# Scores in an attention block: the keys' low parts as one zero-padded matmul, or as two of 64 rows with a PSUM bank per pair of heads

## The chip, the cores and the metric

The kernel runs on one core of a Trainium2 chip. The metric is the device time of one execution in microseconds, the median of several runs. The core has TensorE (matmuls; its weight loads are shown as an engine of their own, PEld, beside PE), VectorE (DVE), ScalarE (ACT), GpSimd (POOL) and SyncE (SP), which here only issues DMAs.

## What is computed

One decoder layer for 512 tokens of width 4096: an RMS norm, one projection to queries (64 heads of 64), keys and values (8 heads of 64) and a gate (4096 wide), attention in a window of 128 tokens with a sink per head, the gate, an output projection, a residual and a final norm.

```python
h = rms_norm(x, norm_g)
q, k, v, z = split(h @ w_in + b_in)              # 4096, 512, 512, 4096 columns
s = einsum(q, k) * 64 ** -0.5                    # each query block of 128 against its own and the block before
s = where(0 <= i_q - i_k < 128, s, -inf)
m = max(max(s), sink)
p = exp(s - m) / (sum(exp(s - m)) + exp(sink - m))
x = x + ((p @ v) * silu(z)) @ w_out + b_out
out = rms_norm(x, final_g)
```

All of it is float32. The kernel's matmuls take operands in the format `fp32r`; it splits each operand into a high part (rounded to `fp32r`) and a low part (the rest), and sums three products: high x high, high x low, low x high.

## The kernel before

**Stages.** The input projection runs over 72 tiles of 128 output columns: for each of the 8 groups one tile with a key and a value head (`kv`), four with queries (`q0` to `q3`, two heads each) and four with the gate (`z0` to `z3`). A tile `acc` is 128 columns x 512 tokens in one PSUM bank and takes 32 steps over the 4096 inputs with three matmuls of 512 columns each (`mm_tile`, all through the helper `mm` at line 97). Weights come by DMA from SyncE's queue and are split on ScalarE and VectorE (`split`, lines 128 and 129). Then the output projection runs over 8 blocks of 512 columns, with the final norm behind it.

**Attention between the projection's matmuls.** The attention of a group is worked off while the projection of the following tiles runs. `tick()` is called after every chunk of 12 projection matmuls, and work that `at()` put down for that tick is issued there. All matmuls are kept in the order in which the program issues them (`tc.keep_in_program_order`), so TensorE's order is written out by hand. `quad` handles two query tiles, that is four heads in two pairs, and puts down for each of the four blocks of 128 tokens (n = 0 to 3): `scores` (three ticks apart), three ticks later `turn` (transposes of the probabilities), and two ticks after that `attend` (the product with the values). So `turn` of a block stands directly ahead of `scores` of the next block in one tick. There are 8 groups x 2 quads x 4 blocks = 64 calls of `scores`.

**The operands of the scores.** `q_tile` makes, from two heads in 128 rows, the tile `q2`: for head h one half of the rows holds the high part and the other half the low part (128 rows, per 64 tokens and head). `qq` collects high parts alone: rows 0 to 63 those of the first query tile of the quad (pair a = 0), rows 64 to 127 those of the second (a = 1). `kv_tile` makes `kh`, the keys' high part, in both halves of the rows, and `kl`, their low part: `kl[0:64, 0]` and the same values in `kl[64:128, 1]`, while the other two quarters hold zeros, written once by two memsets at the start (lines 272 and 273). `kl` is one tile for the whole kernel.

**A call of `scores`.** For each half-block u of 64 queries, the weights are `q2[a]` of 128 rows x 128 columns (two heads x 64 queries), for a = 0 and 1, with `kh` moving: that gives q_high x k_high and q_low x k_high in one matmul. Then one matmul with `qq` as weights and `kl` moving, over both its planes, adds q_high x k_low for both pairs: plane a meets zeros in the rows of the other pair. The result `ps` is 128 x 2 x 2 x 256, two PSUM banks, one per half-block u, both pairs in it. The window of keys has 192 columns, and 64 and 128 in the first block. After it VectorE brings the window into place (`copy_predicated`), takes the maximum, and ScalarE forms the exponentials. `ps` has one buffer.

Of each matmul the chip shows a weight load (LDWEIGHTS, on PEld) and the matmul itself.

Of the kernel before, what the change touches and what calls it, by code (L numbers as in the profile page):

```python
# [8 lines left out]
F32 = mybir.dt.float32  # L9
F32R = mybir.dt.float32r  # L10
I32 = mybir.dt.int32
AF = mybir.ActivationFunctionType
ALU = mybir.AluOpType
AX = mybir.AxisListType

P = 128
D = 4096
S = 512
HD = 64
# [8 lines left out]
QH = P // 2  # L28
# [14 lines left out]
def hybrid_block_kernel(  # L43
# [13 lines left out]
    nc = tc.nc  # L57
# [14 lines left out]
    for h in range(2):  # L72
        rows = mask[h * QH:(h + 1) * QH, 0]
# [22 lines left out]
    def mm(*a, **k):  # L96
        tc.keep_in_program_order(nc.tensor.matmul(*a, **k))  # L97

    def tr(*a, **k):
        tc.keep_in_program_order(nc.tensor.transpose(*a, **k))  # L100
# [5 lines left out]
    def at(slot, fn):  # L106
        clock[1] += 1
        due.append((slot, clock[1], fn))
# [51 lines left out]
    def split_w(raw, j):  # L160
        hi = wpool.tile([P, CW], F32R, name="whi", tag="whi", bufs=WB)
        lo = wpool.tile([P, CW], F32R, name="wlo", tag="wlo", bufs=WB)
        latest[1:] = split(raw[:, j], hi, lo)
        return hi, lo


    with ExitStack() as ph:
        att = ph.enter_context(tc.tile_pool(name="att", bufs=1))
        ps_s = ph.enter_context(tc.tile_pool(name="ps_s", bufs=1, space=PS))
# [76 lines left out]
        def scaled(acc, tag="tmp"):  # L246
            t = att.tile([P, S], F32, name=tag, tag=tag, bufs=1 if tag == "z" else 2)
            nc.vector.tensor_tensor(t, acc, rbc, op=ALU.mult)  # L248
            return t
# [18 lines left out]

        NW = S // QH + 1

        kl = att.tile([P, 2, S], F32R, name="kl")
        nc.vector.memset(kl[0:HD, 1].bitcast(F32), 0.0)
        nc.vector.memset(kl[HD:P, 0].bitcast(F32), 0.0)

        def kv_tile(g, acc):
            t = g * TPG
            b = bcol[:, t:t + 1]
            tmp = scaled(acc)
            kh = att.tile([P, S], F32R, name="kh", tag="kh", bufs=1)
            nc.scalar.activation(kh[0:HD], tmp[0:HD], AF.Identity, bias=b[0:HD])  # L280
            nc.vector.scalar_tensor_tensor(
                kl[0:HD, 0], tmp[0:HD], b[0:HD], kh[0:HD].bitcast(F32), op0=ALU.add, op1=ALU.subtract
            )
            nc.scalar.copy(kh[HD:P], kh[0:HD].bitcast(F32))
            nc.vector.tensor_copy(kl[HD:P, 1], kl[0:HD, 0].bitcast(F32))
            vT = att.tile([P, S], F32, name="vT", tag="tmp", bufs=2)
            nc.scalar.activation(vT, tmp, AF.Identity, bias=b)


            vv = att.tile([P, NW, 2, HD], F32R, name="vv", tag="vv", bufs=1)  # L290
            vw = att.tile([P, NW - 1, 2, HD], F32R, name="vw", tag="vw", bufs=1)
            lo, hi = slice(0, QH), slice(QH, P)

            def values():
                kv = ps_t.tile([P, NB, P], F32, name="pv", tag="pt")
                for n in range(NB):
                    tr(kv[:, n, :], vT[:, n * P:(n + 1) * P], ident)
                pv = kv[:, :, HD:]
                nc.gpsimd.memset(vv[lo, 0].bitcast(F32), 0.0)
                vh, vl = (vv[:, 1::2, i, :] for i in range(2))  # L300
                nc.scalar.copy(vh, pv)
                nc.vector.tensor_tensor(vl, pv, vh.bitcast(F32), op=ALU.subtract)
                nc.gpsimd.tensor_copy(vv[lo, 2::2], vv[hi, 1::2].bitcast(F32))
                nc.gpsimd.tensor_copy(vv[hi, 0:NW - 1:2], vv[lo, 1::2].bitcast(F32))
                nc.gpsimd.tensor_copy(vw[lo], vv[lo, 1:].bitcast(F32))
                nc.gpsimd.tensor_copy(vw[hi], vv[hi, :NW - 1].bitcast(F32))

            at(clock[0] + 1, values)
            return kh, vv, vw
# [28 lines left out]
        def scores(pair, n, q2, qh, kh):  # L338

            ps = ps_s.tile([P, 2, 2, 2 * P], F32, name="ps")
            for u in range(2):
                t0 = n * P + u * QH
                k0 = max(t0 - P, 0)
                o = ps[:, u, :, k0 - (t0 - P):QH + P]
                ks = slice(k0, t0 + QH)  # L350
                for a in range(2):
                    mm(o[:, a], q2[a][:, 2 * n + u], kh[:, ks], start=(a == 0), stop=False)
                mm(o, qh[:, 2 * n + u], kl[:, :, ks], start=False, stop=True)
            if n == 0:
                for u in range(2):
                    nc.vector.memset(ps[:, u, :, 0:P - u * QH], BIG)
            nc.vector.copy_predicated(
                ps[:, :, :, 0:QH], mask.bitcast(I32).unsqueeze(1).to_broadcast([P, 2, 2, QH]),
                ps[:, :, :, P:QH + P],
            )  # L360
            hs = slice(pair, pair + 2)
            nm = small.tile([P, 2, 2], F32, name="nm", tag="nm", bufs=2)
            nc.vector.tensor_reduce(nm, ps[:, :, :, 0:P], axis=AX.X, op=ALU.max, negate=True)
            nc.vector.scalar_tensor_tensor(  # L364
                nm, nm, SCALE, nsink[:, :, hs], op0=ALU.mult, op1=ALU.min
            )
            es = small.tile([P, 2, 2], F32, name="es", tag="es", bufs=2)
            nc.vector.tensor_tensor(es, nm, sink[:, :, hs], op=ALU.add)
            pr = att.tile([P, 2, 2, P], F32, name="prob", tag="prob", bufs=1)
            den = small.tile([P, 2, 2], F32, name="den", tag="den", bufs=2)  # L370
            for u in range(2):
                for a in range(2):
                    nc.scalar.activation(  # L373
                        pr[:, u, a, :], ps[:, u, a, 0:P], AF.Exp, bias=nm[:, u, a:a + 1],
                        scale=SCALE, accum_out=den[:, u, a:a + 1],
                    )
            nc.scalar.activation(es, es, AF.Exp)
            nc.vector.tensor_tensor(den, den, es, op=ALU.add)
            nc.vector.reciprocal(den, den)
            for u in range(2):  # L380
                for a in range(2):
                    nc.vector.tensor_scalar_mul(pr[:, u, a, :], pr[:, u, a, :], den[:, u, a:a + 1])
            return pr
# [43 lines left out]
        def quad(g, i, q2, qh, kh, vv, vw):  # L427
# [5 lines left out]
            def first(n):  # L433
                prs[n] = scores(g * 4 + 2 * i, n, q2, qh, kh)
# [62 lines left out]
        def evacuate(t, acc):  # L497
            g, i = divmod(t, TPG)
            if TILES[i] == "kv":
                kv[0] = kv_tile(g, acc)  # L500
                return
            p = int(TILES[i][1])
            if TILES[i][0] == "q":
                qs.append(q_tile(g, p, acc))
                if p % 2:
                    quad(g, p // 2, (qs.pop(0), qs.pop(0)), qq[0], *kv[0])
            else:
                gate(g, p, acc)
# [22 lines left out]
        for kc, t in ((kc, t) for kc in range(1, NC) for t in range(NPRE)):  # L531
            k2, i = divmod(kc, 2)
            raw = load_w(w_in[t, k2, :, i * CW:(i + 1) * CW], half=i)
            w = split_w(raw, i)
# [114 lines left out]
    for cc in range(NCC):  # L649
# [6 lines left out]
        for kt in range(HOLD, KT) if last else ():  # L656
# [6 lines left out]
            w = held[kt // 2][:, kt % 2]  # L663
            split(raw[:, kt % 2], w[:, 0], w[:, 1])
        for tb in range(NB):
            for kt in range(HOLD, KT) if last else ():
                w = held[kt // 2][:, kt % 2]
# [55 lines left out]
```

## Time and profile before

| | |
|---|---|
| runs | 2414.47, 2414.7, 2414.8 us; median 2414.7 |
| profiled execution | 2414.5 us, its span 2412.5 us, granted clock 0.998 |
| TensorE (PE) | busy 2396.6 us, 99%, 11025 matmuls |
| weight loads (PEld) | busy 1997.2 us, 83% |
| VectorE | busy 1404.3 us, 58% |
| ScalarE | busy 994.0 us, 41% |
| GpSimd | busy 326.1 us, 14% |
| DMA | 274.69 MB, mean 114 GB/s |

The span runs from the first instruction to the last of the profiled execution. Busy time of an engine is the time in which at least one of its instructions is under way; matmuls overlap in a pipeline and their ends are modelled, so starts say more than durations do. Times without a unit in the rows below are microseconds, those of single instructions in a group nanoseconds.

### The profile page before, as it was taken

Reading aid. Unit: us, or ns where it says so; the run is one execution under the profiler, and the core shown is the slowest. Engines: PE = TensorE matmul, PEld = TensorE weight load, DVE = VectorE, ACT = ScalarE, POOL = GpSimd, SP = SyncE. Lnnn points to the kernel's source line nnn. Section 1 sums busy time; section 2 is a strip of 40 time slices with the busy share of each in tenths; the row PEclk is TensorE's granted clock in tenths of the full one; section 3 lists DMA queues with packets and bytes.
Section 4 is the critical chain, followed back from the end, with each engine's and each line's share of the span. In section 5 each row is a group of like instructions: output and inputs, shape, how many; then the busy total and the mean of one; then the engine's idle time right before and its main releaser. Section 6 shows DMA issues by size and latency. Waiting matters only on the chain.

```text
span 2412.5 us, 30330 instructions
## 1 busy us (share of the span) xinstructions
PE 2396.6 (99%) x11025; PEld 1997.2 (83%) x11025; DVE 1404.3 (58%) x2514; ACT 994.0 (41%) x2146; POOL 326.1 (14%) x454
## 2 busy tenths in 40 slices
PE   9999999999999999999999999999999999999998
PEld 7888888888888888888888888888888888888886
DVE  5666465555646555564655556465764664665565
ACT  6643334343433434343343434334444444444444
POOL 2121011110101111010111101010210110110110
PEclk9999999999999999999999999999999999999999
DMA  9522222323232232333222233333632333333335
GB/s 310 179 98 90 95 96 88 105 88 100 93 96 97 88 100 87 103 96 96 96 89 97 87 105 92 101 92 124 234 121 98 123 123 98 127 122 97 122 118 183
DMA packets 82853, 274.69 MB, mean 114 GB/s; under 512 B 9696, under 2 KB 9728, under 8 KB 82704
## 3 DMA queue, kind: packets, MB, share of 16 engines
q1 hardware_dynamic: 71312, 234.93, 30.1%
q0 software_dynamic: 10816, 36.78, 4.4%
q8 instruction: 87, 1.43, 0.2%
q10 hardware_dynamic: 576, 1.05, 0.1%
q14 instruction: 62, 0.51, 0.1%
HBM read 255.94 MB, written 16.78 MB: 113 GB/s over the span
## 4 chain that ended last, share of the span: by engine, by line
PE 99%; DVE 0%; DMA 0%; POOL 0%; issue 0%; ACT 0%; DVEq 0%; POOLq 0%
PE acc L97 94%; PE ps L97 2%; PE po L97 2%; PE pt L100 1%; DMA bcol<-in_b_in 0%; PE pv L100 0%; DVE y L625 0%; POOL wl L399 0%; POOL wh L399 0%; PE pr L97 0%; DVE xl L212 0%; ACT y L645 0%; DVE xb L644 0%; DVE y L621 0%; POOL ww L399 0%
## 5 line engine op out<-in xcount | busy, mean ns | idle before, releaser
L129 DVE TENSOR_TENSOR wlo<-raw,whi 128x512 fp32r<-128x512 f32 x822 | 582.0, 709 | 787.7 <-ACT whi L128 777.9
L128 ACT CAST whi<-raw 128x512 fp32r<-128x512 f32 x822 | 510.9, 622 | 1206.7 <-PE acc L97 1152.6
L97 PE MATMUL acc<-xh,whi 128*128 128x512 f32 x2304 | 900.6, 391 | 1.8 <-ACT xh L211 1.8
L97 PE MATMUL acc<-xl,whi 128*128 128x512 f32 x2304 | 898.3, 390 | 0.7 <-DVE xl L212 0.7
L97 PE MATMUL acc<-xh,wlo 128*128 128x512 f32 x2304 | 898.3, 390 | 0.0
L97 PE MATMUL acc<-whi,gs 128*128 128x512 f32 x1968 | 606.1, 389 | 0.0
L97 PEld LDWEIGHTS acc<-xh,wlo 128*128 128x128 f32 x2304 | 433.1, 188 | 91.0
L97 PEld LDWEIGHTS acc<-xh,whi 128*128 128x128 f32 x2304 | 433.5, 188 | 87.4 <-ACT xh L211 2.3
L97 PEld LDWEIGHTS acc<-xl,whi 128*128 128x128 f32 x2304 | 433.3, 188 | 85.3 <-DVE xl L212 1.1
L97 PEld LDWEIGHTS acc<-whi,gs 128*128 128x128 f32 x1968 | 369.5, 188 | 76.6
L97 PE MATMUL acc<-wlo,gs 128*128 128x512 f32 x984 | 382.9, 389 | 0.0
L97 PEld LDWEIGHTS acc<-wlo,gs 128*128 128x128 f32 x984 | 184.7, 188 | 38.3
L129 DVE TENSOR_TENSOR gs<-g,gs 128x512 fp32r<-128x512 f32 x256 | 192.2, 792 | 0.6 <-ACT gs L128 0.6
L399 POOL TENSOR_SCALAR_AFFINE_SELECT ww<-wh 64x512 fp32r<-64x512 f32 x64 | 42.1, 658 | 829.7 <-ACT wh L395 829.7
L128 ACT CAST gs<-g 128x512 fp32r<-128x512 f32 x256 | 145.8, 617 | 1.6 <-PE acc L97 1.6
L373 ACT ACTIVATE prob<-ps,nm 128x128 f32<-128x128 f32 x256 | 90.4, 365 | 78.9 <-DVE nm L364 75.0
L471 DVE RECIPROCAL e<-e 128x128 f32<-128x128 f32 x128 | 120.7, 945 | 0.6
L637 POOL DMA_DIRECT2D xb<-in_x x32 | 17.3, 540 | 503.5 <-DVE y L647 503.5
L448 ACT COPY ot<-po 64x256 f32<-64x256 f32 x128 | 46.9, 367 | 56.5 <-DVE o L449 40.1
L449 DVE TENSOR_TENSOR o<-po,ot 64x256 f32<-64x256 f32 x128 | 52.8, 413 | 20.5 <-ACT ot L448 19.8
L322 DVE SCALAR_TENSOR_TENSOR q<-tmp,bcol,q 64x512 fp32r<-64x512 f32 x64 | 59.2, 924 | 6.6 <-ACT q L321 5.4
L248 DVE TENSOR_TENSOR tmp<-acc,rbc 128x512 f32<-128x512 f32 x41 | 28.4, 692 | 57.3 <-PE acc L97 56.7
(111 smaller groups left out, 1450.8 us busy)
## 6 DMA issues: line engine op xcount, KB each, us to landing
raw<-in_w_in SPq DMA_DIRECT2D x272, 512.0 KB, 3.5
raw<-in_w_out SPq DMA_DIRECT2D x128, 512.0 KB, 3.6
raw<-in_w_in SPq DMA_DIRECT2D x32, 256.0 KB, 5.4
row<-in_x POOLq DMA_DIRECT2D x16, 512.0 KB, 6.1
gT<-o POOLq DMA_DIRECT2D x32, 256.0 KB, 2.3
g<-gT SPq DMA_DIRECT2D x16, 512.0 KB, 5.8
xb<-in_x POOLq DMA_DIRECT2D x32, 256.0 KB, 4.0
out_y<-y SPq DMA_DIRECT2D x32, 256.0 KB, 3.0
```

Source lines behind the costliest of these rows:

```text
L97: tc.keep_in_program_order(nc.tensor.matmul(*a, **k))
L100: tc.keep_in_program_order(nc.tensor.transpose(*a, **k))
L128: nc.scalar.copy(hi, src),
L129: nc.vector.tensor_tensor(lo, src, hi.bitcast(F32), op=ALU.subtract),
L248: nc.vector.tensor_tensor(t, acc, rbc, op=ALU.mult)
L322: nc.vector.scalar_tensor_tensor(q2[other, :, h, :], tv[own], b[own], q2[own, :, h, :].bitcast(F32), op0=ALU.add, op1=ALU.subtract,)
L373: nc.scalar.activation(pr[:, u, a, :], ps[:, u, a, 0:P], AF.Exp, bias=nm[:, u, a:a + 1], scale=SCALE, accum_out=den[:, u, a:a + 1],)
L399: nc.gpsimd.affine_select(out=out, in_=src.bitcast(F32), fill=0.0, pattern=[[0, 8], [1 if own else -1, QH]], compare_op=ALU.is_ge if own e ...
L448: nc.scalar.copy(ot[own], pq[other, :, :, h, :])
L449: nc.vector.tensor_tensor(ov[own], pq[own, :, :, h, :], ot[own], op=ALU.add)
L471: nc.vector.reciprocal(c, c)
L637: nc.gpsimd.dma_start(xb, x[tb * P:(tb + 1) * P, cs])
```

## The change

`kl` loses its second plane and the zeros: rows 0 to 63 hold the keys' low part and rows 64 to 127 the same again. `ps` is viewed with its first free axis as the pair a, so that a PSUM bank holds one pair with both half-blocks. The four matmuls with `kh` of both half-blocks come first; the first one into each bank (u = 0) starts its accumulation. Then four matmuls with `kl` follow, each with the 64 rows of one pair: weights `qq[rows]` (64 rows x 128 columns), `kl[rows]` moving, into the bank of that pair. What reads `ps` afterwards is written as before.

```diff
-        kl = att.tile([P, 2, S], F32R, name="kl")
-        nc.vector.memset(kl[0:HD, 1].bitcast(F32), 0.0)
-        nc.vector.memset(kl[HD:P, 0].bitcast(F32), 0.0)
+        kl = att.tile([P, S], F32R, name="kl")
...
-                kl[0:HD, 0], tmp[0:HD], b[0:HD], kh[0:HD].bitcast(F32), op0=ALU.add, op1=ALU.subtract
+                kl[0:HD], tmp[0:HD], b[0:HD], kh[0:HD].bitcast(F32), op0=ALU.add, op1=ALU.subtract
...
-            nc.vector.tensor_copy(kl[HD:P, 1], kl[0:HD, 0].bitcast(F32))
+            nc.vector.tensor_copy(kl[HD:P], kl[0:HD].bitcast(F32))
...
-            ps = ps_s.tile([P, 2, 2, 2 * P], F32, name="ps")
+            banks = ps_s.tile([P, 2, 2, 2 * P], F32, name="ps")
+            ps = banks.rearrange("p a u k -> p u a k")
+            windows = []
             for u in range(2):
                 t0 = n * P + u * QH
                 k0 = max(t0 - P, 0)
-                o = ps[:, u, :, k0 - (t0 - P):QH + P]
-                ks = slice(k0, t0 + QH)
+                windows.append((slice(k0 - (t0 - P), QH + P), slice(k0, t0 + QH)))
+            for u, (w, ks) in enumerate(windows):
                 for a in range(2):
-                    mm(o[:, a], q2[a][:, 2 * n + u], kh[:, ks], start=(a == 0), stop=False)
-                mm(o, qh[:, 2 * n + u], kl[:, :, ks], start=False, stop=True)
+                    mm(ps[:, u, a, w], q2[a][:, 2 * n + u], kh[:, ks], start=(u == 0), stop=False)
+            for u, (w, ks) in enumerate(windows):
+                for a in range(2):
+                    rows = slice(a * HD, (a + 1) * HD)
+                    mm(ps[:, u, a, w], qh[rows, 2 * n + u], kl[rows, ks], start=False, stop=(u == 1))
```

## Rows read from the trace of the kernel before

**Rows 1.** The chain that ended last, by engine and by line, whole span.
```profile
PE 99%; DVE 0%; DMA 0%; POOL 0%; issue 0%; ACT 0%; DVEq 0%; POOLq 0%
PE acc L97 94%; PE ps L97 2%; PE po L97 2%; PE pt L100 1%; DMA bcol<-in_b_in 0%; PE pv L100 0%; DVE y L625 0%; POOL wl L399 0%; POOL wh L399 0%; PE pr L97 0%; DVE xl L212 0%; ACT y L645 0%; DVE xb L644 0%; DVE y L621 0%; POOL ww L399 0%
```

**Rows 2.** Busy time by stretch, from 96 to 1710 us, with its header.
```profile
core 0: us, PE busy (x) PEld busy (x) DVE busy (x) ACT busy (x) POOL busy (x), PEclk, DMA share, GB/s
96.00:1710.00 1614.00, 1613.62 (x7584) 1351.04 (x7583) 943.45 (x1813) 621.65 (x1467) 226.29 (x329) 1.00 0.31 99
```

**Rows 3.** TensorE's waits, whole span: us in total, times, longest.
```profile
PE acc L97 <- ACT xh L211: 1.8, 1, 1.8
PE idle L97 <- DVE zero L175: 1.3, 1, 1.3
PE acc L97 <- DVE xl L212: 0.7, 1, 0.7
PE po L97 <- POOL wl L399: 0.4, 1, 0.4
```

**Rows 4.** TensorE's instructions in order (start us, us long): transposes alone.
```profile
331.34 0.39 PE L97 MATMUL acc<-xh,wlo 128*128 128x512 f32 x1
...
332.02 0.39 PE L97 MATMUL acc<-xh,wlo 128*128 128x512 f32 x1
332.25 0.60 PE L100 MATMUL pt<-ident,prob 128*128 128x128 f32 x4
332.60 0.48 PE L97 MATMUL acc<-xh,whi 128*128 128x512 f32 x1
...
333.38 0.40 PE L97 MATMUL acc<-xh,whi 128*128 128x512 f32 x1
```

**Rows 5.** Instructions in order: a later score call behind its transposes.
```profile
393.83 0.88 DVE L382 TENSOR_SCALAR prob<-prob,den 128x128 f32<-128x128 f32 x4
...
396.51 0.39 PE L97 MATMUL acc<-xh,wlo 128*128 128x512 f32 x1
...
396.74 0.60 PE L100 MATMUL pt<-ident,prob 128*128 128x128 f32 x4
...
397.98 0.39 PE L97 MATMUL acc<-xh,whi 128*128 128x512 f32 x1
...
398.66 0.39 PE L97 MATMUL acc<-xh,whi 128*128 128x512 f32 x1
...
398.73 0.42 DVE L357 COPY_PREDICATED ps<-mask,ps 128x256 f32<-128x256 int32 x1
...
399.18 0.69 DVE L363 TENSOR_REDUCE nm<-ps 128x4 f32<-128x512 f32 x1
```

**Rows 6.** Instructions in order: a first score call.
```profile
387.66 0.40 PE L97 MATMUL acc<-xh,wlo 128*128 128x512 f32 x1
...
388.00 0.19 PEld L97 LDWEIGHTS ps<-kl,qq 128*128 128x128 f32 x1
...
388.12 0.30 PEld L97 LDWEIGHTS ps<-kh,q 128*128 128x128 f32 x2
...
388.34 0.19 PEld L97 LDWEIGHTS ps<-kl,qq 128*128 128x128 f32 x1
388.40 0.33 PE L97 MATMUL ps<-kl,qq 128*128 128x256 f32 x1
388.45 0.19 PEld L97 LDWEIGHTS acc<-xh,whi 128*128 128x128 f32 x1
...
389.26 0.39 PE L97 MATMUL acc<-xh,whi 128*128 128x512 f32 x1
```

**Rows 7.** Instructions that write `ps`, whole span: durations ns min/median/max, first and last start.
```profile
L97 PEld LDWEIGHTS ps<-kh,q x256: 187/192/193, 111.2 to 1687.7; 128*128 128x128 f32 x128
L97 PE MATMUL ps<-kh,q x256: 196/275/335, 111.4 to 1687.8; 128*128 128x192 f32 x96, 128*128 128x64 f32 x16, 128*128 128x128 f32 x16
L97 PEld LDWEIGHTS ps<-kl,qq x128: 191/192/193, 111.5 to 1687.8; 128*128 128x128 f32 x128
```

**Rows 8.** VectorE's instructions in order, from the start.
```profile
1.28 0.48 DVE L272 MEMSET kl<- 64x512 f32 x1
1.91 0.48 DVE L273 MEMSET kl<- 64x512 f32 x1
6.43 0.20 DVE L93 TENSOR_SCALAR nbcol<-bcol 128x72 f32<-128x72 f32 x1 [4.03 <-DMA bcol<-in_b_in]
```

## The prediction

> **What bounds the kernel now.** I read the chain of waits first: 99% of the span belongs to TensorE, 94% to the projections' `acc` and 2% to the scores' `ps` [rows 1]. Then the table of stretches over the stage with the attention in it: from 96 to 1710 us TensorE's matmuls are busy for 1613.62 of 1614.00 us, at a granted clock of 1.00, the level of 2.4 GHz [rows 2]. The waits confirm it: four in the whole span, three ahead of the first `acc` matmuls and one, 0.4 us for GpSimd, in this stage [rows 3]. So the time that the change takes on TensorE or gives back there goes into the end one for one, and what it does elsewhere counts only if it makes TensorE wait.
>
> A busy row of TensorE is no price, because rows overlap. I price by starts. Dense `acc` matmuls of 512 columns: 331.34 to 332.02 us is three steps, 0.227 us each [rows 4]. The cost of a burst of other work is then the time from one `acc` matmul to a later one, less 0.227 for each `acc` step in it.
> - Transposes alone: 332.02 to 333.38 is 1.36 us with four `acc` steps: 1.36 - 0.908 = 0.45 us [rows 4].
> - A later score call (n = 1, 2 or 3; there are 48), which always follows four transposes: 396.51 to 398.66 is 2.15 us with four `acc` steps: 1.24, less the transposes' 0.45, is **0.79 us** [rows 5].
> - A first score call (n = 0; there are 16), which stands alone: 387.66 to 389.26 is 1.60 us: **0.69 us** [rows 6].
> Together 48 x 0.79 + 16 x 0.69 = 49.0 us, 2.0% of 2412.5: the chain's share of `ps` [rows 1].
>
> Both calls are six loads and six matmuls, and only the widths differ (64, 64, 128, 128, 128, 256 columns against 192, 192, 384 twice). That the first call, with half the columns, is only 0.10 us shorter shows what sets it: the weight loads. In the first call the loads start at 388.00, 388.12, one more, 388.34 and 388.45: four steps in 0.45 us, **0.112 us a load**, whatever the matmul beside it is [rows 6]. Six of them are 0.67, nearly the whole 0.69. In the later call the four q matmuls of 192 columns (0.080 us at 2.4 GHz) take that slot too, 0.45, and the two of 384 columns (0.160 us) share the other 0.34, 0.17 each: they alone stream longer than a load lasts [rows 5, 7].
>
> **The change part by part.**
> 1. Removed, for each half-block u: one matmul of `qq` with the zero-padded `kl` over 2 x 192 columns, and one load. In a later call that is two slots of 0.17, 0.34 us; in a first call two slots of 0.112, since its matmuls (128 and 256 columns) are no longer than a load.
> 2. Added, for each u: two loads and two matmuls of 64 rows, one per pair of heads, each 192 columns in a later call (0.080 us of stream). Four more slots per call. Every load of the scores is of 128 x 128 [rows 7], so the slot of a 64-row load is not shown, nor whether two of them, in different halves of the array's rows, go side by side. Bounds: four slots of 0.112 if they queue as all loads here do (0.45); two if each pair shares one (0.22); and two of the stream's 0.080 if the loads vanish too (0.16).
>  I take four slots. The nearest row is the load of 128 rows, and the trace has the loads evenly in a row behind one another, never two at once.
>  On this the Trainium skill speaks for and against. "TensorE: Matmul & The Clock Gate", section "LDWEIGHTS (loading the stationary operand)", gives a load columns / 1.2 ns and says that the number of rows doesn't matter: 107 ns by an estimate from it, and the trace's 112 ns agrees for 128 rows; by it alone the sum is four slots. The same page, section "The mechanism" under the packing of small matmuls, says that loads and matmuls of different row groups overlap, with starts some 4 ns apart: by that the sum is two. No run here shows either for 64 rows.
> 3. Forecast for the calls: later, 8 x 0.112 = 0.90 for 0.79, +0.106 us, x 48 = +5.1 us. First, 0.69 + 2 x 0.112 = 0.91, +0.224 us, x 16 = +3.6 us. **Sum +8.7 us.**
> 4. The order: all four q matmuls come first, then the four with `kl`. On TensorE's queue the burst keeps its place. Nothing else is moved past, no DMA is issued in it, and no new wait is added: the first matmul waits for the same bank release, the last signals the same readers.
> 5. A bank per pair instead of a bank per half-block: the tile is as large as before (two banks), and the copy, the maximum and the exponentials read the same number of elements with other strides. I put it at nothing. Its cover: the probabilities are finished at 393.83 + 0.88 = 394.71 us, and the transposes that read them start at 396.74, 2.0 us later [rows 5]. A burst that ends 0.2 us later fits into that, and so does a copy and a maximum that take twice their 0.42 and 0.69 us. With the cover gone, TensorE would wait out the delay in each call, 64 x 0.2 = 13 us for the later burst alone.
> 6. The two memsets of zeros go: 0.48 us each on VectorE at 1.28 and 1.91 us, after which VectorE waits 4.03 us for a DMA [rows 8]. Worth nothing. The writes of `kl` keep their shapes.
>
> The profiled execution took 2414.5 us (span 2412.5 and 2.0 around it), the median of the runs is 2414.7. So 2414.5 + 8.7 = 2423.2, and 0.2 more on the runs' scale: **2423.4 us**.
>
> **Rivals.**
> A. *The pairs run side by side.* Each pair of 64-row matmuls takes one slot: later 6 x 0.112 = 0.67, -0.118 x 48 = -5.7 us; first 6 slots as before, 0. **2409.0 us**; if a pair costs only its stream, 2 x 0.032 x 64 = 4.1 us less, 2404.9. For it: the halves of the rows are separate in `qq` and `kl`, neighbours in the queue go to different banks, and they don't depend on each other. Against it: the loads' even steps in the trace, and that most of the gain must come from the loads, not from the stream, since 192 columns are shorter than a load.
> C. *Side by side, but the array is emptied at each change between 128-row and 64-row form.* There are two changes a call: into the `kl` matmuls and back to `acc`. A q matmul's row lasts 0.275 us from start to end [rows 7], so a matmul that must wait for that end instead of its slot loses 0.275 - 0.112 = 0.163 us; if its load waits too, 0.06 more (388.34 to 388.40 [rows 6]), 0.223. Two per call, 64 calls: 20.9 to 28.5 us, with A's gain **+15.2 to +22.8, 2429.9 to 2437.5 us**. A call already has q, `kl`, transpose and `acc` matmuls in a row without such a hole, but all in one form of 128 rows, so this speaks neither way. It decides from 0.045 us a change (5.7 / 128): above that A's gain is gone.
>  The Trainium skill has this rule, in "TensorEngine Tiling (Array Packing)", section "Key Properties": a change of the tiling mode drains the engine. It gives no price, and no run here shows one.
> D. *Emptied, and no overlap:* +8.7 and 20.9 to 28.5, 2444 to 2452 us.
> E. *Side by side with a cheap change,* 0.02 to 0.08 us each: -3 to +4.5 us, 2411.5 to 2419 us, no change that can be told.
>
> **How the numbers follow.** Chances: the forecast 0.34, A 0.27, C 0.21, E 0.10, D 0.08. The time is the forecast's. A measurement of this kernel can tell 0.2%, 4.8 us, from no change. A lies at -0.24%, so nearly all of it, 0.23, counts as faster; the rest of it and E and the lower edge are no change, 0.16; forecast, C and D are slower, 0.61. The range is 2407 to 2439: it leaves out D, the lowest part of A and the highest of C, some 0.17. The forecast's own range is 2420 to 2427 (a slot of 0.105 to 0.117).
>
> **What would show it.** In the changed profile a call has eight loads and eight matmuls, the last four of 64 x 128. Step 2 is right if the `kl` loads start 0.11 us apart and a later call costs 0.90 by the same reckoning. A shows as two `kl` matmuls that start within 0.03 us, and 0.67 a call. C shows as a hole of 0.15 us or more ahead of the first `kl` matmul and ahead of the `acc` matmul behind the call. If TensorE's waits for other engines grow beyond 1 us, step 5 is wrong. The forecast is wrong if the time is under 2420.

## The result: slower by 0.7%, and by the price of another mechanism than the forecast's

The changed kernel takes **2431.66 us** (median of 6 runs, 2431.06 to 2432.95) against 2414.77 for the kernel before beside it: 16.9 us more, ratio 1.007, 95% interval 1.0059 to 1.0081. "Slower" was forecast, and the time lies in the range of 2407 to 2439. But it is outside the forecast's own 2420 to 2427 and inside rival C's 2429.9 to 2437.5, and the profile shows rival C.

TensorE's waits in the changed kernel (us in total, times, longest) are those of [rows 3] to within 0.4 us, and that one is at the start:

```profile
PE acc L97 <- ACT xh L211: 2.2, 1, 2.2
PE idle L97 <- DVE zero L175: 1.3, 1, 1.3
PE acc L97 <- DVE xl L212: 0.8, 1, 0.8
PE po L97 <- POOL wl L403: 0.4, 1, 0.4
```

The stage with the attention, now 98 to 1728 us, is as full as in [rows 2]: 1629.62 of 1630.00 us busy, at the full granted clock.

```profile
98.00:1728.00 1630.00, 1629.62 (x7709) 1353.39 (x7708) 943.21 (x1812) 621.89 (x1467) 219.21 (x329) 1.00 0.32 98
```

So the time went into TensorE's own work. A later score call of the changed kernel, TensorE and then its loads in order of time (start us, us long), to set beside [rows 5]:

```profile
132.18 0.39 PE L97 MATMUL acc<-xh,wlo 128*128 128x512 f32 x1
132.41 0.60 PE L100 MATMUL pt<-ident,prob 128*128 128x128 f32 x4
132.77 0.67 PE L97 MATMUL ps<-kh,q 128*128 128x192 f32 x4
133.37 0.47 PE L97 MATMUL ps<-kl,qq 64*128 64x192 f32 x4
133.77 0.51 PE L97 MATMUL acc<-xh,whi 128*128 128x512 f32 x1
134.11 0.40 PE L97 MATMUL acc<-xl,whi 128*128 128x512 f32 x1
134.34 0.40 PE L97 MATMUL acc<-xh,wlo 128*128 128x512 f32 x1
134.58 0.39 PE L97 MATMUL acc<-xh,whi 128*128 128x512 f32 x1
```

By the prediction's reckoning: 132.18 to 134.58 is 2.40 us with four `acc` steps, 2.40 - 0.908 - 0.45 = **1.04 us** for 0.79. A first call, to set beside [rows 6]:

```profile
112.87 0.40 PE L97 MATMUL acc<-xh,wlo 128*128 128x512 f32 x1
113.10 0.56 PE L97 MATMUL ps<-kh,q 128*128 128x64 f32 x4
113.59 0.44 PE L97 MATMUL ps<-kl,qq 64*128 64x64 f32 x4
113.96 0.50 PE L97 MATMUL acc<-xh,whi 128*128 128x512 f32 x1
...
114.76 0.39 PE L97 MATMUL acc<-xh,whi 128*128 128x512 f32 x1
```

112.87 to 114.76 less four steps is **0.98 us** for 0.69. Together 48 x 0.25 + 16 x 0.29 = 16.6 us. Summed over the matmuls' starts in all 64 calls of both traces, the calls take 64.82 us in the changed kernel and 48.75 in the kernel before: 16.1 more.

The same later call in narrower windows, which part the merged rows. First the matmuls, then the loads:

```profile
133.16 0.27 PE L97 MATMUL ps<-kh,q 128*128 128x192 f32 x1
...
133.37 0.36 PE L97 MATMUL ps<-kl,qq 64*128 64x192 f32 x2
...
133.56 0.28 PE L97 MATMUL ps<-kl,qq 64*128 64x192 f32 x2
```
```profile
133.07 0.19 PEld L97 LDWEIGHTS ps<-kh,q 128*128 128x128 f32 x1
...
133.37 0.18 PEld L97 LDWEIGHTS ps<-kl,qq 64*128 64x128 f32 x2
...
133.47 0.19 PEld L97 LDWEIGHTS ps<-kl,qq 64*128 64x128 f32 x2
133.76 0.19 PEld L97 LDWEIGHTS acc<-xh,whi 128*128 128x128 f32 x1
```

Two things are to be seen. Each pair starts as one: two loads in the time of one (0.18 us), and two matmuls in 0.36 us that last 0.354 each (durations ns of the same two):

```profile
L97 PE MATMUL ps<-kl,qq x2: 354/354/354, 133.4 to 133.4; 64*128 64x192 f32 x2
```

And the loads, which follow one another at 0.10 to 0.11 us within a form, stand 0.30 us apart from the last q load to the first `kl` pair and 0.29 from the second pair to `acc`: two holes of some 0.18 us over the load's slot. Both end when the last matmul of the old form is nearly through: its row runs from 133.16 to 133.43, and the first `kl` load starts at 133.37; the second pair's rows run from 133.56 to 133.84, and the `acc` load starts at 133.76. In all 128 changes of the trace the new form's first load starts 0.071 to 0.073 us before the modelled end of the last matmul of the old form, whether that has 128 columns or 192. Where the form stays, a load of the 128-row score matmuls starts with at least 0.16 us of the matmul under way still to run.

The profiled execution of the changed kernel took 2432.95 us, 18.45 more than that of before; its span grew by 18.4. Of this, 16.1 is in the calls; most of the rest arises ahead of the first call. From 10.5 to 14.5 us the granted clock was 0.52 in the changed kernel and 0.92 in the kernel before. A third row is that of experiment 1 below, which has the memsets that the change removes and got the full clock as late, so they have no part in it:

```profile
10.50:14.50 4.00, 4.00 (x11) 3.14 (x10) 1.46 (x3) 1.06 (x3) 0.38 (x1) 0.52 1.03 406
```
```profile
10.50:14.50 4.00, 4.00 (x17) 3.23 (x17) 1.44 (x4) 1.24 (x3) 0.00 (x0) 0.92 1.03 409
```
```profile
10.50:14.50 4.00, 4.00 (x11) 3.10 (x10) 1.46 (x3) 1.38 (x3) 0.49 (x1) 0.51 1.02 402
```

Eleven matmuls fall into that stretch in place of 17, and the first score call begins 1.7 us later (113.10 for 111.4). The start differs from trace to trace: the `acc` matmuls go over from 0.43 us a step to 0.23 at 11.1 us in the kernel before, at 14.4 in the changed kernel and in experiment 1, at 13.1 to 13.6 in experiments 2, 3, 4 and 6. Of the change only the memsets lie that early, so I don't count it to the change.

### The profile page after: what moved, and what is told of

Same layout as the page of the kernel before. It is cut to its first block, busy times and chain, and to the rows that moved or that the text cites. A ratio compares the mean times of both kernels' runs of the same rounds, so it can differ in the third digit from the quotient of the medians.

```text
span 2430.9 us, 30569 instructions
## 1 busy us (share of the span) xinstructions
PE 2414.7 (99%) x11153; PEld 2001.1 (82%) x11153; DVE 1404.8 (58%) x2512; ACT 994.5 (41%) x2146; POOL 320.4 (13%) x454
## 4 chain that ended last, share of the span: by engine, by line
PE 99%; DVE 0%; DMA 0%; POOL 0%; issue 0%; ACT 0%; DVEq 0%; POOLq 0%
PE acc L97 94%; PE ps L97 2%; PE po L97 2%; PE pt L100 1%; DMA bcol<-in_b_in 0%; PE pv L100 0%; DVE y L629 0%; POOL wl L403 0%; POOL wh L403 0%; PE pr L97 0%; DVE xl L212 0%; ACT y L649 0%; DVE xb L648 0%; DVE y L625 0%; POOL ww L403 0%
## 5 line engine op out<-in xcount | busy, mean ns | idle before, releaser
L453 DVE TENSOR_TENSOR o<-po,ot 64x256 f32<-64x256 f32 x128 | 52.8, 412 | 20.5 <-ACT ot L452 19.8
```

Source lines behind the costliest of these rows:

```text
L453: nc.vector.tensor_tensor(ov[own], pq[own, :, :, h, :], ot[own], op=ALU.add)
```

## The experiments

Theory C: the pairs run side by side, and each change between the 128-row and the 64-row form costs a hole. Rival B is what was left of the forecast: a 64-row matmul takes a slot like any other, and order and banks cost the rest. The first four were run together, against 2415.45 us of the kernel before.

**1. Order and banks alone, no 64-row form.** The changed kernel, with `kl` in its two zero-padded planes again:

```diff
...
-                    rows = slice(a * HD, (a + 1) * HD)
-                    mm(ps[:, u, a, w], qh[rows, 2 * n + u], kl[rows, ks], start=False, stop=(u == 1))
+                    mm(ps[:, u, a, w], qh[:, 2 * n + u], kl[:, a, ks], start=False, stop=(u == 1))
```

> The changed kernel's order (four matmuls with the keys' high parts first) and its bank per pair, but the product with the low parts as four matmuls of 128 rows against the zero-padded planes: no 64-row form. Theory C (pairs run side by side, and each change between the 128-row and the 64-row form leaves a hole of 0.15 to 0.18 us): eight load slots of 0.112 and no hole, 2414.8 + 8.7 = 2423.5 us. Rival B (order and banks cost what exceeds the forecast, a 64-row matmul takes a slot like any other): as the changed kernel, 2431.7 us.

2425.17 us, ratio 1.0041 (1.0026 to 1.0055): 9.7 us over before, where 8.7 was expected. A later call of it:

```profile
121.99 0.39 PE L97 MATMUL acc<-xh,wlo 128*128 128x512 f32 x1
...
123.08 0.61 PE L97 MATMUL ps<-kl,qq 128*128 128x192 f32 x4
123.53 0.41 PE L97 MATMUL acc<-xh,whi 128*128 128x512 f32 x1
...
124.25 0.40 PE L97 MATMUL acc<-xh,whi 128*128 128x512 f32 x1
```

2.26 - 0.908 - 0.45 = 0.90 us, eight slots of 0.112. Over all 64 calls of its trace the calls take 57.37 us, 8.6 more than before. The forecast's sum is right for this kernel, which isn't the one that was changed to: with the same order and banks, 64 rows in place of 128 cost 16.9 - 9.7 = 7.2 us more.

**2. Four changes of form in place of two.**

```diff
             for u, (w, ks) in enumerate(windows):
                 for a in range(2):
                     mm(ps[:, u, a, w], q2[a][:, 2 * n + u], kh[:, ks], start=(u == 0), stop=False)
-            for u, (w, ks) in enumerate(windows):
                 for a in range(2):
                     rows = slice(a * HD, (a + 1) * HD)
```

> The changed kernel with its matmuls in the order of the half-blocks: two with the high parts, the pair of 64 rows, two with the high parts, the pair of 64 rows. Same instructions, four changes of form a call in place of two. Theory C: two holes more per call, 2 x 0.17 x 64 = 22 us, 2453 us. Rival B (no cost of the change of form): the order of before comes back, at most 2431.7 us.

2452.8 us, ratio 1.0155 (1.0139 to 1.017): 37.4 us over before. The same matmuls in another order cost 20.5 us more than in the changed kernel: 20.5 / 128 = 0.16 us a change. A later call:

```profile
121.83 0.39 PE L97 MATMUL acc<-xh,wlo 128*128 128x512 f32 x1
122.06 0.60 PE L100 MATMUL pt<-ident,prob 128*128 128x128 f32 x4
122.42 0.45 PE L97 MATMUL ps<-kh,q 128*128 128x192 f32 x2
122.80 0.36 PE L97 MATMUL ps<-kl,qq 64*128 64x192 f32 x2
123.08 0.46 PE L97 MATMUL ps<-kh,q 128*128 128x192 f32 x2
123.48 0.36 PE L97 MATMUL ps<-kl,qq 64*128 64x192 f32 x2
123.76 0.50 PE L97 MATMUL acc<-xh,whi 128*128 128x512 f32 x1
...
124.57 0.39 PE L97 MATMUL acc<-xh,whi 128*128 128x512 f32 x1
```

2.74 - 0.908 - 0.45 = 1.38 us. Less six slots, 0.67, that is 0.71 for four changes, 0.18 each; the changed kernel's (1.04 - 0.67) / 2 gives 0.18 too. The cost goes by the number of changes, and each of the 256 changes of this trace has its new load 0.07 us before the modelled end of the last matmul, as in the changed kernel. From the last load of the old form to the first of the new it is 0.23 us behind a matmul of 64 columns, 0.26 behind 128 and 0.29 behind 192, going into the 64-row form. Cost by number and wait by the old form's last matmul together name the mechanism: TensorE lets the old form's last matmul run out before it takes the other form.

**3. One pair left out.**

```diff
...
             for u, (w, ks) in enumerate(windows):
-                for a in range(2):
+                for a in range(1):
                     rows = slice(a * HD, (a + 1) * HD)
```

> The changed kernel, and the product with the keys' low parts is left out for the second pair of heads: two 64-row matmuls a call, both in rows 0 to 63, in place of four. Theory C: the partner rides free (it starts 4 ns later), the holes stay: 2431 us, within 1. Rival B: two slots of 0.112 fewer in 64 calls, -14.3 us, 2417.4 us.

2431.06 us, 15.6 over before, and the changed kernel 16.9: 128 loads and 128 matmuls fewer give back 1.3 us, 0.01 each. The two loads that are left in a call take 0.29 us, where the changed kernel's four, in the first of these rows, take 0.30:

```profile
133.37 0.30 PEld L97 LDWEIGHTS ps<-kl,qq 64*128 64x128 f32 x4
```
```profile
122.46 0.29 PEld L97 LDWEIGHTS ps<-kl,qq 64*128 64x128 f32 x2
```

The partner rides nearly free. Rival B, which asked for 14.3, falls here, and with it the prediction's D, which has no overlap either.

**4. Pair by pair.**

```diff
-            for u, (w, ks) in enumerate(windows):
-                for a in range(2):
+            for a in range(2):
+                for u, (w, ks) in enumerate(windows):
                     rows = slice(a * HD, (a + 1) * HD)
```

> The changed kernel with its 64-row matmuls pair by pair: both half-blocks of pair 0 (rows 0 to 63), then both of pair 1 (rows 64 to 127). Two changes of form as before, but only the middle two neighbours lie in different rows. Theory C: three groups in place of two, one slot of 0.112 more in 64 calls, +7 us, 2439 us. Rival B (nothing runs side by side): 2431.7 us.

2431.34 us, 15.9 over before: no slot more, the expected 2439 was wrong. By its number alone this is rival B's 2431.7; by its rows it is not. The program issues, in a first call, 64 columns and 128 columns of pair 0 and then the same of pair 1. What had started by 112.98 us in such a call, of the `kl` instructions (durations ns, first and last start us):

```profile
L97 PEld LDWEIGHTS ps<-kl,qq x2: 183/183/183, 112.9 to 112.9; 64*128 64x128 f32 x2
L97 PE MATMUL ps<-kl,qq x2: 293/294/294, 112.9 to 112.9; 64*128 64x64 f32 x2
```

Both are of 64 columns, one of each pair. The second overtook the matmul of 128 columns that stands ahead of it in the program. That TensorE was given them in the program's order is not read off directly, but the starts speak for it: in all 64 calls the second load of a first pair starts 6 to 7 ns behind the first, where it is 2 to 4 ns in the changed kernel and in experiment 2, as if one more instruction had been passed. So neighbours needn't lie in different halves; it looks as if each half of the rows works off its own queue.

The next three were run together, against 2415.11 us.

**5. No product with the low parts.**

```diff
...
-            for u, (w, ks) in enumerate(windows):
-                for a in range(2):
-                    rows = slice(a * HD, (a + 1) * HD)
-                    mm(ps[:, u, a, w], qh[rows, 2 * n + u], kl[rows, ks], start=False, stop=(u == 1))
```

> The changed kernel, and the product with the keys' low parts is left out altogether: four matmuls of 128 rows a call, no 64-row form, the banks as changed. If the loss sits in the changes of form alone, a call is four load slots of 0.112: 48 x (0.45 - 0.79) + 16 x (0.45 - 0.69) = -20 us, 2395 us. If the bank layout or the order of the four costs too, it stands above 2397 us.

2397.1 us, ratio 0.9925 (0.9911 to 0.9938). The product thus costs 18.0 us in the kernel before and 18.0 + 16.9 = 34.9 in the changed one. The gain is 2 us short of the slots' sum, just at the bound that was set for a cost of banks and order, and experiment 1 is 1 us over its sum. The calls themselves are not: summed over all 64 of each trace, experiment 5's take 19.9 us less than those of the kernel before, for 20 by the slots, and experiment 1's 8.6 more, for 8.7. So order and banks cost TensorE next to nothing in the calls. The 1 to 2 us lie outside them, at the start and in the `acc` steps behind the later calls; those steps are longer in experiment 7 too, which has the banks and the order of before. What lengthens them stays open.

**6. The pairs twice.**

```diff
+            for i in range(2):
-            for u, (w, ks) in enumerate(windows):
+                for u, (w, ks) in enumerate(windows):
...
-                    mm(ps[:, u, a, w], qh[rows, 2 * n + u], kl[rows, ks], start=False, stop=(u == 1))
+                        mm(ps[:, u, a, w], qh[rows, 2 * n + u], kl[rows, ks], start=False, stop=(i == u == 1))
```

> The changed kernel with its four 64-row matmuls issued twice over (the product with the keys' low parts is added twice): four more of them a call, and no further change of form. A pair that shares one load slot: 2 x 0.112 x 64 = 14 us on 2431.7, 2446 us. No sharing: 4 x 0.112 x 64 = 29 us, 2460 us. If a pair costs the 0.19 us that lie between the starts of the two pairs in the changed kernel's later calls: 24 us, 2456 us.

2447.54 us, 32.4 over before and 15.5 more than the changed kernel: 15.5 / 128 = 0.12 us a pair, near the load's slot of 0.112 and not the 0.19 that lies between the starts of the first two pairs. A later call's eight loads:

```profile
122.91 0.52 PEld L97 LDWEIGHTS ps<-kl,qq 64*128 64x128 f32 x8
```

Four pairs in 0.52 us, with 0.19 for the last load, is (0.52 - 0.19) / 3 = 0.11 us from pair to pair.

**7. The low product in bfloat16, from the kernel before.** If loads set the slots, a shorter load must show without any 64-row form:

```diff
-        kl = att.tile([P, 2, S], F32R, name="kl")
+        kl = att.tile([P, 2, S], mybir.dt.bfloat16, name="kl")
...
-                qq[0] = att.tile([P, S // QH, 2, QH], F32R, name="qq", tag="qq", bufs=1)
+                qq[0] = att.tile([P, S // QH, 2, QH], mybir.dt.bfloat16, name="qq", tag="qq", bufs=1)
```

> The kernel before, zero-padded planes and all, with the operands of the low product alone (qq and kl) in bfloat16. If weight loads set the slots of the narrow matmuls, a shorter load shows in the slot ahead of it: a q matmul of 192 columns falls from 0.112 to at least 0.093 (0.080 of stream and the 0.013 that acc matmuls take over theirs), 2 x 0.019 x 48 = 1.8 us, and up to 2 us more in the first calls: 2411 to 2413 us. If something else sets the slots: 2414.8 us.

**2412.35 us**, ratio 0.999 (0.9981 to 0.9999), 2.8 us under the kernel before and the fastest that computes the whole product; only experiment 5, which leaves the low product out, is shorter. It beats both kernels by little, and it rounds the operands of the low product to bfloat16; what that costs in precision was not measured. Its first call, matmuls and then loads:

```profile
175.54 0.40 PE L97 MATMUL acc<-xh,wlo 128*128 128x512 f32 x1
...
176.26 0.48 PE L97 MATMUL acc<-xh,whi 128*128 128x512 f32 x1
...
177.05 0.39 PE L97 MATMUL acc<-xh,whi 128*128 128x512 f32 x1
```
```profile
175.92 0.10 PEld L97 LDWEIGHTS <-qq 128*128 128x128 bf16 x1
```

The bfloat16 load's row is 0.10 us for 0.19 of [rows 7], and the call 1.51 - 0.908 = 0.60 us for 0.69. The first calls, all loads, gain most. The format of the matmul changes with that of the load, so this run alone doesn't part the two.

## Why the prediction came out right in its sign and wrong in its reason

- **What bounds it, and the reckoning by starts: right.** TensorE takes the difference nearly one for one, and the calls account for 16 of the 16.9 us.
- **Step 2, four slots for the 64-row matmuls: wrong.** They are two: the pairs share a load's slot (experiments 3 and 6). The even steps of the 128-row loads, on which I put my weight, said nothing about loads into different halves of the rows. What I called a load's time is the 0.112 us between starts; a load's row lasts 0.19 us [rows 6], so "never two at once" holds for starts alone.
- **Step 3, +8.7 us: wrong by that and by step 4.** It is the price of the padded form of experiment 1. The right sum has six slots and two changes: 0.67 + 2 x 0.18 = 1.03 for a later call; a first call's changes are shorter, (0.98 - 0.67) / 2 = 0.155, with 128 columns to run out in place of 192 (experiment 2 has the same order behind 64, 128 and 192).
- **Step 4, "no new wait is added": wrong, and this is the step that costs.** No semaphore's wait came, as the unchanged waits show, but the order brings two changes of form a call, and TensorE stops at each without any wait in the profile.
- **Rival C: right,** its price, from a single row, 0.163 to 0.223 us for a measured 0.155 to 0.18, so near its lower end and in part under it, and its point of decision, 0.045. The rule of the Trainium skill beside it ("TensorEngine Tiling (Array Packing)", "Key Properties") agrees with experiment 2. I gave C 0.21 against 0.34 because no row of before showed a change; none could, with all matmuls in one form.
- **Steps 5 and 6: right in that nothing waits** on the new bank layout or on the memsets; on TensorE itself the order and the layout cost next to nothing in the calls (8.6 us for 8.7 in experiment 1).
- **The sign is luck.** Two errors pull against each other: the shared slots are worth -5.7 us where +8.7 was put, and the changes of form cost 48 x 0.36 + 16 x 0.31 = 22.2 us where nothing was put. With a change of form under 0.045 us the kernel would have been faster. That the time lies in the wide range is owed to rival C, which the range took in.

## What to carry to other kernels

A pair of 64-row matmuls in place of a zero-padded one gains what the padded one takes over a load's slot, here 0.17 - 0.112 = 0.06 us, or 0.05 by experiment 6's 0.12 a pair, and a visit to the 64-row form costs two changes, 0.36 us. By an estimate from these rows that takes six or seven such pairs per visit, and a call has two. Where matmuls stream for less than the 0.112 us of a load's slot, count loads, not columns; where the precision allows, a shorter load may give something back, here 2.8 us.

## What the runs showed of the hardware that was not expected

- Matmuls in different halves of the rows overtake one another: experiment 4's two 64-column matmuls start together although a 128-column one stands between them in the program, as far as the program's order is the order given to TensorE. "TensorE: Matmul & The Clock Gate" of the Trainium skill, section "The mechanism", has matmuls in strict order; here the trace decides otherwise.
- A change of form shows in no wait: TensorE's row is busy for 1629.62 of 1630.00 us while 64 x 2 holes of about 0.17 us, 22 us, are in it. The last matmul's row, 0.27 us long, covers the hole behind it. Only the starts show them.
